# A decoder trunk on one core: the last down products of each feed-forward layer, the first three begun over chunks 0 to 3 of their input and finished over chunks 4 and 5

## The chip, the cores and the metric

The kernel runs on one core of a Trainium2 chip. The metric is device time in microseconds (us) of one execution, the median of several runs. A profile shows one execution in detail. Engine names: PE multiplies matrices (PEld is its loading of weights), DVE, ACT and POOL are the vector, scalar and general-purpose engines, SP issues most of the DMAs.

## What is computed

One inference step of a two-layer trunk over 512 prompt tokens and 32 sample tokens (544 columns), width 1024. Each layer has a mixer (a convolution in layer 0, an attention in layer 1) and then this feed-forward part, whose last line is what the change touches:

```python
def conv_ffn(h, past, w_gate, w_up, w_dw, b_dw, w_down):
    g = h @ w_gate
    ext = jnp.concatenate([past, g], axis=1)
    g_conv = causal_dwconv(ext, w_dw, b_dw)
    out = (jax.nn.silu(g_conv) * (h @ w_up)) @ w_down
    return out, ext[:, -(FFN_CONV_WIDTH - 1):]
...
    x = x + out            # layer 0: then the norm and mixer of layer 1
...
y = rms_norm(x, norm_final)  # layer 1: then the final norm, and y is stored
```

The hidden width is 2816, 22 chunks of 128.

## The kernel before

Activations lie transposed: 128 channels on the partitions, tokens along the free axis, cut in two stretches, SA (columns 0 to 255) and SB (256 to 543, 288 wide). Every matrix product is made of three matmuls per chunk of 128 inputs, because both operands are split into a high and a low part: high weights by high input, high weights by low input, low weights by high input (L459, L460, L461 in `gemm`). A weight block of 128 output channels sits in a slot. ACT writes its high part `whi` (L369) and DVE its low part `wlo` (L372) from a raw block that SP has loaded (L332); when the second block of a raw has been split, its buffer takes the next load.

`ffn` walks over the 22 hidden chunks in passes of 4, 6, 6 and 6 (`PASSES`). For a pass it computes gates and ups, multiplies them into a hidden tile `h`, and splits that into `HH` (ACT, L1596) and `HL` (DVE, L1597), one chunk of 544 columns at a time. Those are the inputs of the down products, which add into the residual `xT`. A list scheduler (`Plan`) sets the order of all this by estimated costs, except for the down products of the last pass, 8 groups for 8 output chunks, which are written out after the plan in program order. There nk is 6: each group runs over hidden chunks 16 to 21, called chunks 0 to 5 below. On every engine the instructions run in the order in which the program issues them.

In layer 0 those last products go through `Wide.stream`, first all 8 groups on SA, then all 8 on SB. Three further slots are prepared in the SA stream after groups 0, 1 and 2. In layer 1 they go through `add_group` and `run_group`, 4 groups at a time: SA then SB for output chunks 0 to 3, SB then SA for 4 to 7. Each group sums into a bank of PSUM (`acc`, four of them in turn); DVE then adds the bank to `xT` (L1687 in layer 0, L1239 in layer 1: the eviction), and a norm object is fed. `Norm.feed` has ACT square the chunk and DVE add it up. In layer 1 `Final.feed` also has ACT write the scaled chunk `xg` (L1725), and PE transposes it (`yt`, L1740) some steps later.

What is to be done "some steps later" waits in a deque `side`. `gemm` takes one entry off it at each of four places in a group: with nk = 6 these come after chunks 1, 2, 4 and 5.

## Time and profile before

| what | value |
|---|---|
| time, median of 3 runs | 1290.41 us (1287.6 to 1290.61) |
| the profiled execution's own time | 1289.36 us |
| its span, first to last instruction | 1287.7 us |
| PE busy | 1270.2 us, 99% of the span |
| DVE busy | 980.4 us, 76% |
| ACT busy | 713.5 us, 55% |
| mean granted PE clock | 0.997 of full speed |
| last down products of layer 0, SA stream | 555.0 to 573.7 us |
| last down products of layer 1 | 1235.5 us to the end of the last group near 1279 us |

A line of the timeline reads: start in us, duration in us, engine, line of the kernel, operation, output<-input, shape, and in brackets how long the engine had been idle and what released it. Matmuls overlap in PE: a matmul of 256 columns is listed with 0.28 us, but a new one starts every 0.12 us, so the spacing of the starts is what one costs.

### The profile page before, as it was taken

To read this page: it belongs to the slowest core of one execution; us is meant where nothing else is said; L and a number is where in the kernel's file an instruction comes from. 1 tells how busy PE (TensorE), PEld (TensorE's weight loads), DVE (VectorE), ACT (ScalarE), POOL (GpSimd) and SP (SyncE) were. 2 spreads that over 40 slices of the span, in tenths; PEclk is the share of its full clock that TensorE was granted. 3 is DMA by queue.
4 is the path that set the end of the run, shared out by engine and by line. 5 is a ranking of instruction groups with operands and counts; after the bars stand their busy time and mean duration, and the time that the engine had idled before them with its cause. 6 is when DMAs were issued, how large, how long until landed. Compare 5 with 4: busy or idle time off the path is not lost.

```text
span 1287.7 us, 26497 instructions
## 1 busy us (share of the span) xinstructions
PE 1270.2 (99%) x10860; PEld 1215.5 (94%) x10860; DVE 980.4 (76%) x1671; ACT 713.5 (55%) x1440; POOL 152.4 (12%) x289
## 2 busy tenths in 40 slices
PE   9999999999999999999999999999999999999997
PEld 8997789999999999999988888889999999999997
DVE  6899875979987877768366586756988987887864
ACT  7596574645644545445366587754645555455453
POOL 4000014101001000000142123100111011000000
PEclk9999999999999999999999999999999999999999
DMA  8465233133232223244553445333133233233221
GB/s 225 123 175 140 83 100 114 34 92 107 91 117 91 91 93 115 67 133 141 175 159 120 140 140 175 104 113 99 50 100 92 93 114 115 67 116 94 80 76 70
DMA packets 119402, 142.38 MB, mean 111 GB/s; under 512 B 5357, under 2 KB 110469, under 8 KB 119010
## 3 DMA queue, kind: packets, MB, share of 16 engines
q1 hardware_dynamic: 110350, 111.89, 28.1%
q0 software_dynamic: 8640, 28.78, 7.1%
q8 instruction: 85, 1.39, 0.5%
q14 instruction: 35, 0.29, 0.1%
q10 hardware_dynamic: 292, 0.02, 0.0%
HBM read 129.34 MB, written 12.18 MB: 110 GB/s over the span
## 4 chain that ended last, share of the span: by engine, by line
PE 85%; DVE 10%; issue 2%; ACT 1%; DMA 1%; DVEq 0%; POOL 0%; ACTq 0%; POOLq 0%
PE acc L1545 5%; PE acc L1543 5%; PE acc L1544 5%; PE acc L700 4%; PE acc L701 4%; PE acc L702 3%; PE acc L459 3%; PE acc L460 3%; PE acc L461 3%; PE tr L1544 3%; PE tr L1543 3%; PE tr L1545 3%; PE av L1341 3%; PE acc L1969 3%; PE av L1343 3%; PE av L1342 3%
## 5 line engine op out<-in xcount | busy, mean ns | idle before, releaser
L372 DVE TENSOR_TENSOR wlo<-raw,whi 128x1024 fp32r<-128x1024 f32 (+2 forms) x245 | 257.4, 1052 | 46.0 <-ACT whi L369 44.5
L369 ACT CAST whi<-raw 128x1024 fp32r<-128x1024 f32 (+2 forms) x245 | 223.5, 914 | 117.1 <-PE av L1342 24.6
L700 PE MATMUL acc<-XH,whi 128*128 128x288 f32 (+1 forms) x384 | 114.5, 298 | 0.0
L701 PE MATMUL acc<-XL,whi 128*128 128x288 f32 (+1 forms) x384 | 110.9, 289 | 0.1
L702 PE MATMUL acc<-XH,wlo 128*128 128x288 f32 (+1 forms) x384 | 110.4, 288 | 0.1
L1969 PE MATMUL acc<-XH,whi 128*128 128x256 f32 (+1 forms) x264 | 82.8, 314 | 0.6 <-ACT XH L2274 0.6
L1543 PE MATMUL acc<-TH,whi 128*128 128x272 f32 x288 | 82.9, 288 | 0.0
L1545 PE MATMUL acc<-TH,wlo 128*128 128x272 f32 x288 | 82.8, 288 | 0.0
L1544 PE MATMUL acc<-TL,whi 128*128 128x272 f32 x288 | 82.7, 287 | 0.0
L1579 ACT COPY G<-acc 128x272 f32<-128x272 f32 (+1 forms) x72 | 26.7, 371 | 94.9 <-PE acc L1545 94.9
L1341 PE MATMUL av<-HH,whi 128*128 128x288 f32 x256 | 76.2, 298 | 0.2
L1970 PE MATMUL acc<-XL,whi 128*128 128x256 f32 (+1 forms) x264 | 76.2, 289 | 0.1
L1971 PE MATMUL acc<-XH,wlo 128*128 128x256 f32 (+1 forms) x264 | 75.9, 287 | 0.0
L1342 PE MATMUL av<-HL,whi 128*128 128x288 f32 x256 | 75.5, 295 | 0.0
L1343 PE MATMUL av<-HH,wlo 128*128 128x288 f32 x256 | 75.3, 294 | 0.0
L700 PEld LDWEIGHTS acc<-XH,whi 128*128 128x128 f32 x384 | 72.2, 188 | 2.8 <-issue 1.6
L701 PEld LDWEIGHTS acc<-XL,whi 128*128 128x128 f32 x384 | 72.3, 188 | 1.0 <-DVE XL L952 0.3
L702 PEld LDWEIGHTS acc<-XH,wlo 128*128 128x128 f32 x384 | 72.2, 188 | 0.3 <-DVE wlo L372 0.3
L1341 PE MATMUL tr<-HH,whi 128*128 128x256 f32 x256 | 71.9, 281 | 0.0
L1342 PE MATMUL tr<-HL,whi 128*128 128x256 f32 x256 | 71.9, 281 | 0.0
L1343 PE MATMUL tr<-HH,wlo 128*128 128x256 f32 x256 | 71.5, 279 | 0.0
L1482 DVE SCALAR_TENSOR_TENSOR cv<-G,fprm,cv 128x560 f32<-128x560 f32 x88 | 69.5, 797 | 0.5
(405 smaller groups left out, 4395.5 us busy)
## 6 DMA issues: line engine op xcount, KB each, us to landing
raw<-in_ffn_w_gate_dram SPq DMA_DIRECT2D x22, 1024.0 KB
raw<-in_ffn_w_up_dram SPq DMA_DIRECT2D x22, 1024.0 KB, 5.4
raw<-in_ffn_w_down_dram SPq DMA_DIRECT2D x24, 768.0 KB, 4.7
raw<-in_attn_w_qkv_dram SPq DMA_DIRECT2D x12, 1024.0 KB, 7.9
raw<-in_conv_w_in_dram POOLq DMA_DIRECT2D x6, 1024.0 KB, 7.8
rep<-glu SPq DMA_DIRECT2D x36, 142.0 KB, 3.7
raw<-in_conv_w_out_dram POOLq DMA_DIRECT2D x4, 1024.0 KB, 6.0
raw<-in_ffn_w_down_dram SPq DMA_DIRECT2D x8, 512.0 KB, 3.4
```

What stands on the lines that cost most here:

```text
L369: act.copy(hi[:, k, :], src[:, k])
L372: dve.tensor_tensor(lo[:, k, :], src[:, k], hi[:, k, :], op=ALU.subtract)
L700: pe.matmul(o, hi[:, k, :], XH[:, k, c0:c0 + n], start=(k == 0), stop=False)
L701: pe.matmul(o, hi[:, k, :], XL[:, k, c0:c0 + n], start=False, stop=False)
L702: pe.matmul(o, lo[:, k, :], XH[:, k, c0:c0 + n], start=False, stop=(k == NC - 1))
L1341: pe.matmul(o, hi[:, j + k, :], xh, start=(start and k == 0), stop=False, **kw)
L1342: pe.matmul(o, hi[:, j + k, :], xl, start=False, stop=False, **kw)
L1343: pe.matmul(o, lo[:, j + k, :], xh, start=False, stop=(stop and k == len(xs) - 1), **kw)
L1543: pe.matmul(o, hi[:, j + k, :], xh, start=(start and k == 0), stop=False, **kw)
L1544: pe.matmul(o, hi[:, j + k, :], xl, start=False, stop=False, **kw)
L1545: pe.matmul(o, lo[:, j + k, :], xh, start=False, stop=(k == 3), **kw)
L1969: pe.matmul(o, hi[:, k, :], XH[:, k, c0:c0 + n], start=(k == 0), stop=False)
```

## The change

`AHEAD = 3`. For the first stretch of the last products, `begin` takes three of the four banks and runs groups 0, 1 and 2 over chunks 0 to 3 (`ready = nk - 2`), 12 matmuls each, one group after the other. Then the groups are run as before, but 0, 1 and 2 only over chunks 4 and 5, 6 matmuls each; from group 3 on nothing is split. This is done for SA in layer 0 and for SA of output chunks 0 to 3 in layer 1. No instruction is added or removed. The begun parts take nothing off `side`, so that groups 0, 1 and 2 have two places each instead of four.

```diff
+AHEAD = 3
-    def gemm(pt, st, slot, xh, xl, places=None):
+    def gemm(pt, st, slot, xh, xl, places=None, ks=(0, NF)):
-        for k in range(nk):
+        for k in range(max(0, ks[0]), min(nk, ks[1])):
+    def begin(n, ready, s0, st, xh, xl):
+
+        pts = [bank("acc", uid("acc")) for _ in range(n)]
+        for i, pt in enumerate(pts):
+            gemm(pt, st, s0 + i, xh, xl, None, (0, ready))
+        return pts
...
+        begun = begin(AHEAD, ready, s0, order[0], xh, xl) if ready else []
...
-                pt = bank("acc", uid("acc"))
+                k0 = ready if begun else 0
+                pt = begun.pop(0) if begun else bank("acc", uid("acc"))
...
-                gemm(pt, st, s0 + i, xh, xl, places if hooked else None)
+                gemm(pt, st, s0 + i, xh, xl, places if hooked else None, (k0, NF))
...
-                last.stream(st)
+                last.stream(st, ready=0 if st is SB else nk - 2)
...
-                add_group(c4, HH, HL, after, hooked=True, order=(SB, SA) if c4 else (SA, SB))
+                add_group(c4, HH, HL, after, hooked=True, order=(SB, SA) if c4 else (SA, SB), ready=0 if c4 else nk - 2)
```

Place 1, PE in layer 0, the start of the last products. `acc_7003` is the bank of group 0, `acc_7028` before and `acc_7004` after that of group 1, `acc_7005` that of group 2; a bracket names the engines whose semaphores a matmul waits for. Before, the end of chunk 3 and then chunks 4 and 5 of group 0:

```order
L459 MATMUL acc_7003<-HH_3021,whi_6882 128x256
L460 MATMUL acc_7003<-HL_3022,whi_6882 128x256
L461 MATMUL acc_7003<-HH_3021,wlo_6883 128x256
L459 MATMUL acc_7003<-HH_3021,whi_6882 128x256 [waits Activation_49]
L460 MATMUL acc_7003<-HL_3022,whi_6882 128x256 [waits DVE_49]
L461 MATMUL acc_7003<-HH_3021,wlo_6883 128x256
L459 MATMUL acc_7003<-HH_3021,whi_6882 128x256 [waits Activation_49]
L460 MATMUL acc_7003<-HL_3022,whi_6882 128x256 [waits DVE_49]
L461 MATMUL acc_7003<-HH_3021,wlo_6883 128x256
L459 MATMUL acc_7028<-HH_3021,whi_6918 128x256
```

Now, the end of chunk 3 of group 2, and chunk 4 of group 0 behind it (the lines are one higher):

```order
L460 MATMUL acc_7005<-HH_3021,whi_6952 128x256
L461 MATMUL acc_7005<-HL_3022,whi_6952 128x256
L462 MATMUL acc_7005<-HH_3021,wlo_6953 128x256
L460 MATMUL acc_7003<-HH_3021,whi_6882 128x256 [waits Activation_49]
L461 MATMUL acc_7003<-HL_3022,whi_6882 128x256 [waits DVE_49]
L462 MATMUL acc_7003<-HH_3021,wlo_6883 128x256
L460 MATMUL acc_7003<-HH_3021,whi_6882 128x256 [waits Activation_49]
```

The four waits for `HH` and `HL` of chunks 4 and 5 stand 24 matmuls later on PE. DVE, ACT, POOL and SP have the same rows in the same order there as before.

Place 2, PE in layer 1, the transposes of the first chunk. `xg` is output chunk 0 after its eviction, scaled by ACT; `yt` are banks for the transposes. Before, in group 1 (`acc_15164`), 15 matmuls behind the end of group 0:

```order
L461 MATMUL acc_15164<-HH_11157,wlo_15056 128x256
L1740 MATMUL yt_15180<-ident,xg_15159 128x128 [waits Activation_49]
L1740 MATMUL yt_15181<-ident,xg_15159 128x128
L459 MATMUL acc_15164<-HH_11157,whi_15055 128x256
L460 MATMUL acc_15164<-HL_11158,whi_15055 128x256
```

Now, in group 2 (`acc_15140`), 9 matmuls behind the end of group 0, of which six finish group 1 (`acc_15139`):

```order
L462 MATMUL acc_15139<-HH_11157,wlo_15056 128x256
L460 MATMUL acc_15140<-HH_11157,whi_15089 128x256
L461 MATMUL acc_15140<-HL_11158,whi_15089 128x256
L462 MATMUL acc_15140<-HH_11157,wlo_15090 128x256
L1752 MATMUL yt_15205<-ident,xg_15185 128x128 [waits Activation_49]
L1752 MATMUL yt_15206<-ident,xg_15185 128x128
L460 MATMUL acc_15140<-HH_11157,whi_15089 128x256
```

The transposes of the next chunks, and the copies of transposed rows on DVE and ACT (`yrow`), move behind by up to 18 matmuls; from the second group of output chunks 4 to 7 on, every engine has its old order.

More of the change, by code (lines that the diff above doesn't have):

```diff
@@ L472, in take_due, with run_group @@
             side.extend(due.popleft())
-    def run_group(n, xh, xl, evac, hooked=False, order=(SA, SB)):
+    def begin(n, ready, s0, st, xh, xl):
[3 more added lines that the diff above has]
+        return pts
+    def run_group(n, xh, xl, evac, hooked=False, order=(SA, SB), ready=0):
         s0 = slot_no[0]
         slot_no[0] += n
+        begun = begin(AHEAD, ready, s0, order[0], xh, xl) if ready else []
         for st in order:
@@ L499, in __init__, with stream @@
             self.cm, self.pool = open_pool(uid("more"))
-        def stream(self, st, hooked=True):
+        def stream(self, st, hooked=True, ready=0):
             last = st is SB
+            begun = begin(AHEAD, ready, self.s0, st, self.xh, self.xl) if ready else []
             for i in range(NC):
-                pt = bank("acc", uid("acc"))
+                k0 = ready if begun else 0
+                pt = begun.pop(0) if begun else bank("acc", uid("acc"))
                 places = [[some]] * 4
@@ L507, in stream @@
                     places[0] = [take_due, some]
-                gemm(pt, st, self.s0 + i, self.xh, self.xl, places if hooked else None)
+                gemm(pt, st, self.s0 + i, self.xh, self.xl, places if hooked else None, (k0, NF))
                 if not last and i < self.lead:
@@ L1229, in tile_trunk, with add_group @@
     due.append(nrm.steps(SB))
-    def add_group(c4, xh, xl, norm, bias_row=None, hooked=True, order=(SA, SB)):
+    def add_group(c4, xh, xl, norm, bias_row=None, hooked=True, order=(SA, SB), ready=0):
         def evac(i, st, pt):
@@ L1243, in evac @@
                 norm.feed(st, c)
-        run_group(4, xh, xl, evac, hooked=hooked, order=order)
+        run_group(4, xh, xl, evac, hooked=hooked, order=order, ready=ready)
     def ffn(l, before, after):
```

## The prediction

> **What bounds the kernel now.** The page's head and its chain of work that ended last come first.

> ```profile
> span 1287.7 us, 26497 instructions
> PE 1270.2 (99%) x10860; PEld 1215.5 (94%) x10860; DVE 980.4 (76%) x1671; ACT 713.5 (55%) x1440; POOL 152.4 (12%) x289
> PE 85%; DVE 10%; issue 2%; ACT 1%; DMA 1%; DVEq 0%; POOL 0%; ACTq 0%; POOLq 0%
> ```

> PE is the bound nearly everywhere. A change of order in PE's work can win only what PE waits, and the view of waits, for PE, says how much of that is due to the inputs in question:

> ```profile
> PE acc L460 <- DVE HL L1597: 2.1, 4, 0.9
> ```

> Four waits of matmul L460 for `HL`, 2.1 us together. The timeline of PE shows the two of layer 0; the first row is the first matmul of group 0, the last one the first of the SB stream:

> ```profile
> 555.04 0.36 PE L459 MATMUL acc<-HH,whi 128*128 128x256 f32 x1
> 555.24 0.28 PE L460 MATMUL acc<-HL,whi 128*128 128x256 f32 x1
> ...
> 556.54 0.28 PE L459 MATMUL acc<-HH,whi 128*128 128x256 f32 x1
> 556.99 0.39 PE L460 MATMUL acc<-HL,whi 128*128 128x256 f32 x1 [0.17 <-DVE HL L1597]
> 557.21 0.28 PE L461 MATMUL acc<-HH,wlo 128*128 128x256 f32 x1
> 557.33 0.28 PE L459 MATMUL acc<-HH,whi 128*128 128x256 f32 x1
> 558.49 0.39 PE L460 MATMUL acc<-HL,whi 128*128 128x256 f32 x1 [0.88 <-DVE HL L1597]
> 558.72 0.28 PE L461 MATMUL acc<-HH,wlo 128*128 128x256 f32 x1
> ...
> 573.69 0.29 PE L459 MATMUL acc<-HH,whi 128*128 128x288 f32 x1
> ```

> From 558.72 to 573.69 there are 127 starts without a wait: 14.97 / 127 = 0.118 us each. That is the unit below. What PE waits for is made by ACT and DVE, in this order:

> ```profile
> 556.21 0.72 DVE L1597 TENSOR_TENSOR HL<-h,HH 128x544 fp32r<-128x544 f32 x1
> 556.38 0.64 ACT L1596 CAST HH<-h 128x544 fp32r<-128x544 f32 x1
> 556.85 0.95 DVE L372 TENSOR_TENSOR wlo<-raw,whi 128x768 fp32r<-128x768 f32 x1
> 557.72 0.72 DVE L1597 TENSOR_TENSOR HL<-h,HH 128x544 fp32r<-128x544 f32 x1
> 559.04 0.42 DVE L1687 TENSOR_TENSOR xT<-acc,xT 128x256 f32<-128x256 f32 x1 [0.60 <-PE acc L461]
> ```

> `HL` of chunk 4 ends at 556.93, `HH` of chunk 5 at 557.02, `HL` of chunk 5 at 558.44, held up by a `wlo` between the two. None of these waits for the down products, so they stay where they are when PE does other work meanwhile.

> Layer 1 has the same picture:

> ```profile
> 1235.72 0.28 PE L460 MATMUL acc<-HL,whi 128*128 128x256 f32 x1
> ...
> 1237.02 0.28 PE L459 MATMUL acc<-HH,whi 128*128 128x256 f32 x1
> 1237.47 0.39 PE L460 MATMUL acc<-HL,whi 128*128 128x256 f32 x1 [0.17 <-DVE HL L1597]
> ...
> 1237.81 0.28 PE L459 MATMUL acc<-HH,whi 128*128 128x256 f32 x1
> 1238.97 0.38 PE L460 MATMUL acc<-HL,whi 128*128 128x256 f32 x1 [0.88 <-DVE HL L1597]
> 1239.20 0.28 PE L461 MATMUL acc<-HH,wlo 128*128 128x256 f32 x1
> ```

> **The change part by part.** *The two waits of layer 0.* Counted by starts and not by idle time, they cost more than the view of waits says. 556.54 to 556.99 is 0.45, 0.33 above the unit; the next start comes 0.22 later, 0.10 above; 557.33 to 558.49 is 1.16, 1.04 above; the next 0.23, 0.11 above. Sum 1.58 us. The 0.10 behind each wait goes with it, since there PE starts up again from an empty pipe.

> They go if the input is there when PE now comes to it. 36 matmuls stand ahead instead of 12. Counted from the second at 555.24, the matmul that needs `HL` of chunk 5 is the 41st and would start at 555.24 + 39 x 0.118 = 559.84, and `HL` is ready at 558.44: 1.4 us to spare. For chunk 4 (38th, 559.49 against 556.93) it is 2.6 us. So both waits go whole: -1.58 us.

> *What is late next in layer 0.* Group 0 ends later. Its last matmul, at 558.72 so far, is the 42nd and starts at 559.96; its eviction, 0.32 behind that (558.72 to 559.04), moves from 559.04 to 560.28. Its bank is next used by group 4, whose first matmul is the 73rd, at 563.6: 2.9 us of cover for a 0.42 us eviction. Groups 0, 1 and 2 now end 0.71 apart (6 x 0.118) and not 2.1, and between their evictions DVE has the three `wlo` of the slots 5, 6 and 7 to make, 0.95 each as above. So the three evictions and three `wlo` take DVE from 560.28 to about 564.4 (3 x 0.42 + 3 x 0.95 = 4.1). Slot 5 is first needed by the 91st matmul, at 565.7, slot 7 by the 127th at 570. Cost nothing; without that cover PE would wait what DVE is behind.

> SP's next load, the first of the qkv weights, waits for the first of these `wlo`, so it moves from 560.36 to about 561.6:

> ```profile
> 560.36 0.37 SPq L332 DMA_DIRECT2D raw<-in_attn_w_qkv_dram  x1
> raw<-in_attn_w_qkv_dram SPq DMA_DIRECT2D x8, 1024.0 KB, 8.6
> 577.12 1.03 ACT L369 CAST whi<-raw 128x1024 fp32r<-128x1024 f32 x1
> ```

> With 8.6 us to landing (median of these loads, second row) it is there at 570.2. The cast that reads it would come 1.58 earlier than 577.12, at 575.5. Cover 5.3 us, cost nothing. POOL's queue and its DMAs are not touched.

> *Does the gain of layer 0 reach the end?* After the SA stream the chain that ended last runs over DVE until PE takes over again:

> ```profile
> 576.28 0.47 DVE xT L1687
> 592.16 0.40 PE acc L459
> ```

> It enters DVE with the eviction of the first SB group, which waits for PE, so that the norm behind it, and all that follows up to layer 1, starts earlier with PE. I take the whole 1.58.

> *Layer 1.* The same sum, 0.33 + 0.10 + 1.04 + 0.11 = 1.58 us (the restart rows are as in layer 0). `HL` of chunk 5 is needed at 1235.72 + 39 x 0.118 = 1240.32, and its wait so far ended at 1238.97 at the latest: 1.35 to spare. But the transposes now come nearer to what they read:

> ```profile
> 1239.51 0.42 DVE L1239 TENSOR_TENSOR xT<-acc,xT 128x256 f32<-128x256 f32 x1 [0.59 <-PE acc L461]
> 1239.97 0.51 ACT L1725 ACTIVATE xg<-xT,prm 128x256 f32<-128x256 f32 x1 [1.09 <-DVE xT L1239]
> 1240.39 0.40 ACT L1726 ACTIVATE sq<-xT 128x256 f32<-128x256 f32 x1
> 1241.09 0.38 PE L1740 MATMUL yt<-ident,xg 128*128 128x128 f32 x2
> ```

> Group 0's last matmul started at 1239.20, the eviction 0.31 later, `xg` 0.46 after that and ended 0.51 on: 1.28 us in all, and the transposes came 1.89 after that matmul. Now that matmul is the 42nd, at 1240.43, so `xg` ends at 1241.71. Nine matmuls stand between, so the transposes could start at 1240.43 + 10 x 0.118 = 1241.61. They wait 0.1, and with the hand-over from ACT to PE (`HL` ended at 558.44, its matmul started at 558.49) some 0.15 to 0.2. Bounds: nothing at all, and 0.5 if the square (0.40 behind `xg` on ACT) had to be done too. I take 0.2, nearest to the rows' own sum. The next chunk's transposes come 9 matmuls into group 3, over 0.9 us after their `xg`; later ones have moved away from what they read. The final stretch has its old order and starts from PE:

> ```profile
> 1273.14 0.51 PE ms L1759 x6
> ```

> so it shifts as a whole. The row copies on DVE and ACT that move behind an eviction there fill no queue that PE waits for: cost nothing.

> *Sum.* 1.58 + 1.58 - 0.2 = 2.96 us off. The profiled execution's own time is 1289.36 (span 1287.7 and 1.7 around it), which gives 1286.4. The median of the runs, 1290.41, is 1.05 above it, which gives 1287.45. I go from their middle, 1289.9: 1286.9 us, 0.23% less.

> [...] Changing banks costs PE nothing in this trace, with `av` and `tr` two banks of products that are open side by side:

> ```profile
> 548.87 0.29 PE L1545 MATMUL av<-XH,wlo 128*128 128x272 f32 x1
> 549.00 0.29 PE L1543 MATMUL tr<-TH,whi 128*128 128x272 f32 x1
> ```

> 0.13 us from one to the other, as within a bank. [...]

> **The rivals.** B: layer 0's gain is lost on the way, because something between 592 and 1235 us runs by its own clock (a DMA or a POOL gather). For it: 15% of the chain is not PE's. Against it: the chain comes back to PE each time. Then only layer 1 gains: 1289.9 - 1.38 = 1288.5.

> C: the change doesn't do what it says, as a wait for chunk 4 or 5 still stands ahead of the begun groups, or `HL` comes later than now. For it: nothing but that DVE's chain ahead is tight (556.21 to 558.44 without a gap). It would have to slip by 1.4 us. Then 1289.9.

> D: slower, by the clock. At the kernel's start PE ran at half speed, later at full:

> ```profile
> 1.30 4.23 PE L994 MATMUL warm<-zero 128*128 128x256 bf16 x19 [1.30 <-DVE zero L634]
> 8.31 1.91 PE L994 MATMUL warm<-zero 128*128 128x256 bf16 x16
> ```

> 4.23 / 19 = 0.223 against 1.91 / 16 = 0.119 us for 256 columns: 0.103 more for each. If the 54 matmuls of groups 0 to 2 ran so in both layers, that is 108 x 0.103 = 11.1 - 2.96 = 8.2 slower, 1298.1. It decides from 29 slow matmuls on (2.96 / 0.103). [...]

> E: more than the sum, if PE's wait for an eviction in the SB stream of layer 0 also goes:

> ```profile
> PE acc L459 <- DVE xT L1687: 1.1, 1, 1.1
> ```

> 1289.9 - 2.96 - 1.1 = 1285.8. Against it: that wait is the end of the DVE chain from 576.28, which keeps its distance to PE.

> **How the numbers follow.** Chances: my sum 0.68, B 0.12, C 0.05, D 0.04, E 0.11. The runs before spread over 3.0 us (1287.6 to 1290.61), so half of that to either side of 1286.9 is my sum's own range, 1285.4 to 1288.4. To leave out no more than 2 in 10 I reach down below E, to 1284.8, and up to between B and C with that scatter, 1290.2. A measurement of this kernel can tell about 0.3%, 3.9 us, from no change. My sum lies 0.9 us short of that, so scatter carries some one in five of its cases over the line (0.14); with most of E that is 0.23 for faster. Slower is D, 0.04. The rest, 0.73, is within 0.3%.

> **What the profile after would show.** PE's starts from group 0 to group 3 of the SA stream 0.12 apart with no wait for `HL`; the stream from its first matmul to the first of SB 17.1 us long and not 18.65 (573.69 - 555.04). In layer 1 one short wait of a `yt` transpose for `xg`, 0.1 to 0.2. The time from layer 0's last SB matmul to layer 1's first down product unchanged; if it is longer by what layer 0 won, B is right. Spacings of 0.2 in groups 0 to 2 would be D, a wait for `HL` at the 38th or 41st matmul C. I am wrong in size if the restart of 0.1 behind each wait returns without a wait, which would take 0.4 from the sum.

## The result, and the profile after

The changed kernel took 1285.64 us (median of 9 runs, 1284.88 to 1289.31) against 1289.45 us for the kernel before next to it (9 runs, 1287.6 to 1291.52): a ratio of 0.9973, 95% interval 0.9964 to 0.9982, so 0.27% faster. Forecast were 1286.9 us and 0.23%. The profiled execution took 1284.92 us. The head of its page:

```profile
span 1283.2 us, 26496 instructions
PE 1267.9 (99%) x10860; PEld 1213.6 (95%) x10860; DVE 979.9 (76%) x1671; ACT 713.7 (56%) x1440; POOL 152.9 (12%) x289
```

One of the nine runs, that of 1289.31, is 3.7 us above the median, at a mean granted clock of 0.996; the other eight have 0.998.

The span is 4.5 us shorter, and the forecast had 2.96. Both traces hold 10860 matmuls, so the n-th start of one can be set against the n-th start of the other; "shift" below is after less before, read off at places by the time they have before. In the experiments it is the step in this difference at the place named.

| place (us, before) | 534 | 560 | 576 | 620 | 843 | 869 | 1234 | 1248 | 1279 |
|---|---|---|---|---|---|---|---|---|---|
| shift (us) | -0.07 | -1.65 | -1.63 | -1.59 | -1.58 | -3.12 | -3.10 | -4.45 | -4.48 |

Three steps, then: 1.58 at layer 0's last products, 1.53 near 859 us, and 1.35 at layer 1's last products. The first and the third are the change, 2.93 together. The second stands at a place that the change doesn't touch.

The view of waits of after, for PE, has no `HL` any more. The wait of the SB stream for an eviction is still there (the lines of `gemm` moved by 1, those behind it by up to 12):

```profile
PE acc L460 <- DVE xT L1699: 1.1, 1, 1.1
...
PE acc L462 <- DVE wlo L373: 0.7, 1, 0.7
PE av L2277 <- DVE XL L2287: 0.7, 1, 0.7
PE acc L1981 <- ACT XH L2286: 0.6, 1, 0.6
```

The timeline of after, in order of time, answers to the rows of the forecast. The first matmul of group 0, then those that take chunk 4 and 5 of `HL` (the 38th and 41st), the eviction of group 0 with the first `wlo` behind it, SP's load, the third of these `wlo`, the first matmul of the SB stream and the cast that reads SP's load:

```profile
554.97 0.36 PE L460 MATMUL acc<-HH,whi 128*128 128x256 f32 x1
555.17 0.28 PE L461 MATMUL acc<-HL,whi 128*128 128x256 f32 x1
...
559.44 0.28 PE L461 MATMUL acc<-HL,whi 128*128 128x256 f32 x1
559.56 0.28 PE L462 MATMUL acc<-HH,wlo 128*128 128x256 f32 x1
559.68 0.28 PE L460 MATMUL acc<-HH,whi 128*128 128x256 f32 x1
559.80 0.28 PE L461 MATMUL acc<-HL,whi 128*128 128x256 f32 x1
...
560.24 0.42 DVE L1699 TENSOR_TENSOR xT<-acc,xT 128x256 f32<-128x256 f32 x1 [1.87 <-PE acc L462]
560.58 0.95 DVE L373 TENSOR_TENSOR wlo<-raw,whi 128x768 fp32r<-128x768 f32 x1
561.56 0.37 SPq L333 DMA_DIRECT2D raw<-in_attn_w_qkv_dram  x1
563.47 0.95 DVE L373 TENSOR_TENSOR wlo<-raw,whi 128x768 fp32r<-128x768 f32 x1
572.05 0.30 PE L460 MATMUL acc<-HH,whi 128*128 128x288 f32 x1
575.49 1.03 ACT L370 CAST whi<-raw 128x1024 fp32r<-128x1024 f32 x1
```

The second start is 0.20 behind the first, as it was before (555.04 and 555.24). From there on no start is more than 0.12 behind the one ahead, and the stream from first to first is 17.08 us long. In layer 1 the transposes wait once:

```profile
1238.43 0.28 PE L462 MATMUL acc<-HH,wlo 128*128 128x256 f32 x1
1238.71 0.44 PE L1752 MATMUL yt<-ident,xg 128*128 128x128 f32 x2
1238.90 0.36 PE L460 MATMUL acc<-HH,whi 128*128 128x256 f32 x1
1239.11 0.29 PE L461 MATMUL acc<-HL,whi 128*128 128x256 f32 x1
```

The step near 859 us is one of the clock. The stretches of before there, with the columns of us, then for PE, PEld, DVE, ACT and POOL the busy time and number of instructions, then the granted PE clock, DMA share and GB/s:

```profile
855.57:858.98 3.41, 2.04 (x15) 1.47 (x16) 1.07 (x4) 0.94 (x4) 0.00 (x0) 1.00 0.01 5
858.98:862.40 3.42, 3.42 (x19) 3.42 (x18) 1.61 (x4) 1.21 (x3) 0.00 (x0) 0.50 0.00 0
```

and of after at the same work:

```profile
852.18:855.60 3.42, 2.73 (x43) 2.31 (x39) 0.29 (x1) 0.57 (x3) 0.00 (x0) 1.00 0.26 112
855.60:859.01 3.41, 2.67 (x20) 2.27 (x19) 1.75 (x6) 1.18 (x4) 0.00 (x0) 1.00 0.00 0
859.01:862.42 3.41, 3.41 (x28) 3.41 (x27) 1.34 (x4) 0.89 (x3) 0.00 (x0) 1.00 0.02 5
```

Before, PE ran at half clock for 3.41 us, behind a stretch of equal length in which it was busy 60% of the time: layer 1's attention ends there, and PE waits 0.69 us for an `XL` and 0.61 us for an `XH`:

```profile
856.19 0.66 PE L2265 MATMUL av<-w,vtok 128*64 128x128 f32 x8 [0.69 <-DVE XL L2275]
858.00 0.38 PE L1969 MATMUL acc<-XH,whi 128*128 128x256 f32 x1 [0.61 <-ACT XH L2274]
```

After has the same two waits (0.69 and 0.61), but they fall into two stretches, 80% and 78% busy, and there is no half clock. Is this step part of what the change does, or luck of one execution? The second half of the experiments is about that. A stretch of half clock lowers the mean clock of an execution by 0.0013 (half of 3.41 in 1285). In the 14 profiles the mean is 0.997 in the three with such a stretch inside the program, and 0.998 or 0.999 in the others. So the runs can be sorted by it: at 0.997 or less ("low"), or above. The mean does not say where in the execution a stretch stands; only a profile does.

### The profile page after: what moved, and what is told of

The parts are those of the page before. It is cut to its first block, busy times and chain, and to the rows that moved or that the text cites. A ratio compares the mean times of both kernels' runs of the same rounds, so it can differ in the third digit from the quotient of the medians.

```text
span 1283.2 us, 26496 instructions
## 1 busy us (share of the span) xinstructions
PE 1267.9 (99%) x10860; PEld 1213.6 (95%) x10860; DVE 979.9 (76%) x1671; ACT 713.7 (56%) x1440; POOL 152.9 (12%) x289
## 4 chain that ended last, share of the span: by engine, by line
PE 84%; DVE 11%; issue 2%; ACT 1%; DMA 1%; DVEq 0%; SPq 0%; POOL 0%; ACTq 0%; POOLq 0%
PE acc L1557 5%; PE acc L1555 5%; PE acc L1556 5%; PE acc L712 4%; PE acc L713 4%; PE acc L714 3%; PE acc L460 3%; PE acc L462 3%; PE acc L461 3%; PE tr L1557 3%; PE tr L1556 3%; PE tr L1555 3%; PE av L1353 3%; PE acc L1981 3%; PE av L1355 3%; PE av L1354 3%
## 6 DMA issues: line engine op xcount, KB each, us to landing
raw<-in_ffn_w_gate_dram SPq DMA_DIRECT2D x22, 1024.0 KB
raw<-in_ffn_w_up_dram SPq DMA_DIRECT2D x22, 1024.0 KB
raw<-in_attn_w_qkv_dram SPq DMA_DIRECT2D x12, 1024.0 KB
raw<-in_conv_w_in_dram POOLq DMA_DIRECT2D x6, 1024.0 KB, 7.9
raw<-in_conv_w_out_dram POOLq DMA_DIRECT2D x4, 1024.0 KB, 5.8
```

## Experiments: the parts of the change

**Layer 0 alone.**

```diff
-add_group(c4, HH, HL, after, ..., ready=0 if c4 else nk - 2)
+add_group(c4, HH, HL, after, ...)
```

> The begun groups in layer 0 only. Both theories: PE's starts at layer 0's last products lie 1.58 us nearer together, and layer 1 is as before. Theory (grid): the half-clock stretch of 3.41 us that the profile of before has at 859 us comes when a lull in PE's work falls wholly into one window of a grid that is fixed to the program's start; 1.58 us earlier the lull is split over two windows, so that the stretch is gone (another 1.53 us). Then the span is 1284.6 (1287.7 - 1.58 - 1.53) and the runs lie 3.1 us below those runs of before that have the stretch, 1.6 below those that have not. Rival (chance): the stretch comes and goes by itself, whatever the shift; then the mean gain is 1.6 us and this kernel has the stretch as often as before.

1286.36 us, ratio 0.9984 (0.9975 to 0.9993). None of 11 runs was low, against 13 of 33 of the kernel before beside them, and the profile has no half clock inside the program and a span of 1284.7. That speaks against chance, and for the place of the lull. The shift is -1.59 at layer 0's last products and 0.0 at layer 1's, where the two waits are left:

```profile
PE acc L461 <- DVE HL L1609: 1.1, 2, 0.9
```

**Layer 1 alone.**

```diff
-last.stream(st, ready=0 if st is SB else nk - 2)
+last.stream(st)
```

> The begun groups in layer 1 only. Both theories: nothing moves up to 1235 us, then 1.58 - 0.22 = 1.36 us are won, the 0.22 being a wait of the first transposes for their scaled chunk. Theory (grid): up to layer 1 PE stands on the grid as before, so the half-clock stretch at 859 us is there as often as in before, and the span is 1286.3 in a profile that has it. The gains of this and of the run with layer 0 alone then sum to the whole gain of the change. Rival (chance): the stretch is there in some other share of the runs.

1287.93 us, ratio 0.9991 (0.9982 to 1.0). The shift is 0 at layer 0 and -1.35 at layer 1, so that the two halves, 1.59 and 1.35, add up to the whole. Low runs came, 8 of 11, as the grid theory asked. But its half clock at 859 us isn't in the profile, though that is one of the low ones: there the one such stretch begins at 157.62 us (shown in the last section), and the two waits at the end of the attention lie in two stretches that are 80% and 78% busy. So a low run need not have its stretch at the attention.

**Two groups begun and not three.** `AHEAD = 2`.

> Two groups begun instead of three, in both layers. The last HL is ready at 558.44 in layer 0; the matmul that needs it is then the 29th, at 558.43, so PE waits 0.05 us (hand-over) and perhaps starts up again for 0.1: 1.42 to 1.58 us won per layer instead of 1.58. In layer 1 the first transposes stand 12 matmuls behind the end of group 0 instead of 9 (1.42 us; the scaled chunk takes 1.28 us), so the 0.2 us wait for it is gone. Theory: PE at the last products -1.45 in layer 0 and -1.45 in layer 1, the whole within 0.2 us of the changed kernel. Rival (three are needed, because the waits need more room than the starts say): a wait of over 0.3 us for HL is left in each layer, and the gain is under 1.2 us per layer.

1286.02 us, ratio 0.9976 (0.9967 to 0.9985). The view of waits lists none for `HL` here either; the shifts are -1.42 and -1.40. What the third group bought is seen in the starts at the matmul that takes `HL` of chunk 5, the 29th here, 0.05 and 0.10 above the unit:

```profile
559.40 0.28 PE L460 MATMUL acc<-HH,whi 128*128 128x256 f32 x1
559.57 0.39 PE L461 MATMUL acc<-HL,whi 128*128 128x256 f32 x1
559.79 0.28 PE L462 MATMUL acc<-HH,wlo 128*128 128x256 f32 x1
```

That is the 0.05 and the 0.1 of the expectation. In layer 1 the same is lost, and the `yt` transposes, 12 matmuls behind the end of group 0, don't wait.

**Only chunk 5 held back.** `ready = nk - 1` in both places.

> The changed kernel with only chunk 5 held back (ready = nk - 1): groups 0, 1 and 2 begin with 15 matmuls each and end with 3. Theory: the matmuls for chunk 4 of group 0 come as early as before the change, so that wait stays with 0.33 + 0.10 us, and only that of chunk 5 goes, 1.04 + 0.11 = 1.15 us in each layer. In layer 1 the first yt transposes now come 12 matmuls behind the end of group 0 and not 9, 0.35 us more room, so their wait of 0.2 goes too: -2.3 us against the kernel before, in two steps of 1.15. Rival: DVE is what sets it, and a wait removed at chunk 4 comes back elsewhere, so that holding back one chunk is worth as much as two (2.9), or the split in itself costs something, which 18 changes of group instead of 6 would show as less than 2.0.

1286.16 us, ratio 0.9981 (0.9972 to 0.999). The shifts are -1.17 and -1.10. What is left is chunk 4's wait, with 0.44 to its matmul and 0.23 from there to the next, where before had 0.45 and 0.22:

```profile
556.16 0.28 PE L460 MATMUL acc<-HH,whi 128*128 128x256 f32 x1
556.60 0.39 PE L461 MATMUL acc<-HL,whi 128*128 128x256 f32 x1 [0.17 <-DVE HL L1609]
556.83 0.28 PE L462 MATMUL acc<-HH,wlo 128*128 128x256 f32 x1
```

By the steps in the trace, 2.27 together, the theory's 1.15 for chunk 5, and so 0.43 for chunk 4, hold, and the rival (2.9, or under 2.0) falls. The median alone would not say so: it lies 1.6 us under that of before's runs above 0.997, 1287.80.

**The input earlier instead of the matmul later.** In the kernel before, the `wlo` that stands between the two `HL` is issued behind the second:

```diff
...
+            keep = f2 + 2 == NF
...
-                low_h(f2 + i, k0, hs[i])
+            lows = [low_h(f2 + i, k0, hs[i]) for i in range(2)]
+            if keep:
+                prepare(slots[3] + SPLIT_BUFS, lows)
```

> The kernel before with one DVE instruction moved in each layer: the wlo that stands between HL of chunk 4 and HL of chunk 5 comes behind HL of chunk 5. PE's order is that of before. Theory: HL of chunk 5 then starts when HH of chunk 5 is ready (557.02 in layer 0) and not when that wlo has ended (557.72 as the start of HL), 0.65 us earlier, so PE's wait for it shrinks from 1.04 to about 0.4, the rest stays: -0.65 us in each layer, -1.3 us together. The eviction of group 0 then waits some 0.2 to 0.4 us for the wlo, which nothing feels. Rival: HL of chunk 5 is bound by HH or by h, and PE waits as before: 0. Or the wlo behind it comes late for PE's group in that slot, and the gain is lost again: 0 or above.

1286.91 us, ratio 0.9988 (0.9979 to 0.9997). The shifts are -0.56 and -0.66, where -0.65 each was expected. The timeline:

```profile
556.95 0.73 DVE L1598 TENSOR_TENSOR HL<-h,HH 128x544 fp32r<-128x544 f32 x1 [0.22 <-ACT HH L1597]
557.13 0.28 PE L459 MATMUL acc<-HH,whi 128*128 128x256 f32 x1
557.60 0.95 DVE L372 TENSOR_TENSOR wlo<-raw,whi 128x768 fp32r<-128x768 f32 x1
557.73 0.39 PE L460 MATMUL acc<-HL,whi 128*128 128x256 f32 x1 [0.33 <-DVE HL L1598]
557.96 0.28 PE L461 MATMUL acc<-HH,wlo 128*128 128x256 f32 x1
```

Now `HL` waits for `HH`, 557.13 to 557.73 is 0.48 above the unit, and the restart behind it is unchanged. So DVE's order was 0.6 of the 1.58. Beginning three groups is worth more, because it also covers the 1.0 us that the two inputs still cost PE in this order.

## Experiments: the half clock

**The attention later.** To the kernel before, 12 matmuls are added in layer 0, so that all of layer 1 comes 1.6 us later:

```diff
+                if last and i == 0 and self.hold:
+                    for _ in range(12):
+                        pe.matmul(pt[:, :st[1]], W.w[self.s0][0][:, 0, :], self.xh[:, 0, st[0]:st[0] + st[1]],
+                                  start=True, stop=False, skip_group_check=True)
                 gemm(pt, st, self.s0 + i, ...)
```

> The kernel before, with 12 more matmuls of 288 columns at the head of layer 0's SB stream (their sums are overwritten): 12 x 0.133 = 1.6 us more work on PE. Theory (grid): PE's lull moves from 853.5-858.9 to 855.1-860.5 us, over two windows of the grid, the half-clock stretch at 859 us is gone (-1.53), and the kernel with more work is not slower than before where before has the stretch: 0.1 us, span 1287.8. Rival (chance): 1.6 us slower, span 1289.3, with the stretch as often as before.

1289.53 us, ratio 1.001 (1.0001 to 1.0019): the added work cost 1.58 us where it stands, and the median rose by 0.7 only (by 1.6 over before's runs above 0.997, 1287.92). There is no half clock near 859 us in the profile, and none of 11 runs was low, against 13 of 33 runs of before. But the clock does not step at times fixed to the span's start: a stretch of half clock begins at 858.98 us in the profile of before, and at 857.47 in that of the changed kernel with 12 matmuls (below), 1.51 us apart, where a stretch lasts 3.41. So this run alone could not say whether the place mattered.

**The changed kernel again.**

> The changed kernel once more, unchanged. Theory: the gain is what the waits for HL cost by starts, 1.58 us in layer 0 and 1.36 us in layer 1 (1.58 less 0.22 for the wait of the first yt transposes), 2.94 us; what the first comparison showed beyond that (3.8 us between the medians) are executions of the kernel before that lost 1.5 us to a stretch of half granted clock. Then the runs of both kernels with a mean clock of 0.998 lie 2.5 to 3.2 us apart, and runs at 0.997 or less lie 1.3 to 2 us above those of their own kernel. Rival 1: the change also keeps the clock up by itself, because PE pauses less; then the changed kernel has next to no run at 0.997 or less, again, while the kernel before has a third or more of them. Rival 2: the change is worth 3.5 us or more at equal clock; then the distance at 0.998 is 3.5 or more.

1284.66 us (5 runs, 1284.53 to 1284.93), ratio 0.9967 (0.9954 to 0.998). None was low, of before's 29 runs 17. The runs of before above 0.997 have a median of 1287.80, so at equal clock the change is worth 3.1 us, beside 2.94 by the shifts; before's low runs have 1289.42, 1.6 more. The theory's distance holds and rival 2 falls. Its 1.3 to 2 us for a low run could be seen in the kernel before alone; the changed kernel's one low run, in the first comparison, is 3.7 above the median of its own runs there, more than one stretch explains. Rival 1's count came in too: the changed kernel does have next to no low runs. The same kernel took 1285.64 us in the first comparison, so medians of different groups of runs can lie 1 us apart.

**Work in the pause.** The kernel before with six zero matmuls where PE waits for `XH`:

```diff
-    zero = conv.tile([P, 2 * P], BF16, name="zero")
+    zero = base.tile([P, 2 * P], BF16, name="zero")
...
+                if fill and k == NC - 1:
+                    for _ in range(6):
+                        pe.matmul(o, zero[:, :P], zero[:, :n], start=False, stop=False)
```

> The kernel before with six more matmuls of 256 columns (zero weights by zeros, added into an open bank, so that the sums stay the same) in a pause of PE at the end of layer 1's attention: PE had nothing from 857.24 to 858.00 there, waiting for XH. In the profile of before half granted clock set in at 858.98, behind a stretch of 3.41 us in which PE was busy 60% of the time. Theory: such a low stretch is what brings the half clock, and with 0.7 us more work it is 80%; then the profile has no half clock near 859, no or few runs at a mean clock of 0.997 or less, and the median is that of before's runs at 0.998, some 1 us under before's median if these are again a third or more of its runs. The six cost 0 to 0.1 us. Rival: the half clock comes from elsewhere (a level over many us, another place in the program such as the convolution); then the share of runs at 0.997 or less is as in before, and the median is 0 to 0.2 us above it.

1288.34 us, ratio 0.9997 (0.9988 to 1.0006); none of 11 was low, of before's 29 beside them 17. The six cost nothing in the trace (shift +0.24 ahead of them, -1.29 behind, where 1.53 is the missing half clock), but the median is 0.5 above that of before's runs above 0.997, and so only 0.6 under before's whole. The stretch that was 60% busy, between two steps of the clock, is 80% now (second row):

```profile
852.46:855.87 3.41, 3.26 (x44) 2.88 (x42) 0.00 (x0) 0.11 (x1) 0.00 (x0) 1.00 0.74 311
855.87:859.28 3.41, 2.73 (x22) 2.05 (x23) 1.07 (x4) 0.86 (x4) 0.00 (x0) 1.00 0.01 5
```

**The changed kernel with the pause put back, and moved by a whole period.** The 12 matmuls above, now in the changed kernel; then 26 of them (3.4 us) in the changed kernel, and in the kernel before; then the 12 and the six zero matmuls together.

> The changed kernel with 12 matmuls of 288 columns more on PE, into the bank of the first SB group of layer 0's last products ahead of its own (that group clears the bank, so the sums stay the same). All of layer 1 comes 1.5 to 1.6 us later by it, that is where it was before the change. Open is why so many runs of the kernel before, and so few of the changed one, have a stretch of half clock. Theory: the clock is set anew every 3.41 us, at times that lie within about 1 us the same from the start of each execution, and only if one such time falls in the 0.6 us in which the 3.41 us behind it hold the pause at the end of the attention does the half clock come; the change moved that pause by 1.6 us out of it. Then a third or more of these runs are at a mean clock of 0.997 or less, as of before, and the median is 1287 to 1288. Rival 1: those times are free of the program's start; then about 0.6 / 3.41 = 18% of the runs, one to three of eleven, of this kernel as of any other. Rival 2: the change of layer 0 itself keeps the clock up; then none, and 1286.2 to 1286.6.

> The same with 26 matmuls, 3.4 to 3.5 us, one period of the clock's steps. Theory of times that keep to the program's start: the pause comes to the same place in the period as in the changed kernel, so that no or one run is at 0.997 or less; median 1288.1 to 1288.5. Rival 1, free times: one to three of eleven. Were half the runs low here as in the last kernel, the added matmuls would be the cause, and not where the pause falls.

> The kernel before with the 26 matmuls. Theory of times that keep to the program's start: the pause is one period later and so at the same place in the period as in the kernel before, a third or more of the runs at 0.997 or less; median 1291.5 to 1292.5. Rival 1: one to three of eleven. Rival 2, that layer 0 as it was before brings the half clock: as before too, a third or more, so this run parts theory from rival 1 alone.

> The changed kernel with the 12 matmuls of 288 columns in layer 0 and with the six zero matmuls in the pause at the end of layer 1's attention. Theory: the pause no longer holds 0.7 us without work, so wherever it falls no half clock comes: none of the runs at 0.997 or less, median 1286.2 to 1286.8. If the half clock comes from elsewhere: the same share of low runs as in the kernel with the 12 matmuls alone.

With the pause back at its old place, 5 of 11 runs were low (1287.17 us, ratio 0.999, 0.9981 to 0.9999), and its profile shows the half clock again:

```profile
854.06:857.47 3.41, 2.08 (x22) 1.26 (x18) 1.02 (x4) 0.96 (x4) 0.00 (x0) 1.00 0.01 5
857.47:860.88 3.41, 3.31 (x15) 3.31 (x16) 0.90 (x3) 0.83 (x2) 0.00 (x0) 0.50 0.00 0
```

With the pause also filled, none of 11 was low (1287.95 us, ratio 0.9999, 0.999 to 1.0008). With 26 matmuls the changed kernel had none in 11 (1289.35 us, ratio 1.0006, 0.9997 to 1.0015), and the kernel before 3 of 5 (1295.08 us, ratio 1.0061, 1.0048 to 1.0075). All kernels in one table, by how far the pause stands from its place in the kernel before, as their profiles have it:

| kernel | pause moved by (us) | low runs |
|---|---|---|
| before (13 of 33, 17 of 29, 13 of 27) | 0 | 43 of 89 |
| layer 1 alone | 0 | 8 of 11 |
| change, 12 matmuls | 0.0 | 5 of 11 |
| before, 26 matmuls | +3.4, one period | 3 of 5 |
| `wlo` behind `HL` | -0.5 | 3 of 12 |
| only chunk 5 | -1.1 | 0 of 11 |
| two groups | -1.4 | 1 of 11 |
| layer 0 alone; change (two groups of runs) | -1.6 | 0 of 11; 1 of 14 |
| before, 12 matmuls | +1.6 | 0 of 11 |
| change, 26 matmuls | +1.8 | 0 of 11 |
| filled: before; change, 12 matmuls | 0; +0.9 | 0 of 11; 0 of 11 |

Free times (18% for each kernel) don't fit 43 of 89 beside 2 of 69 for the six kernels whose pause stands 1.1 to 1.8 off. That the change itself keeps the clock up by having fewer waits falls too: with the same waits removed, the low runs are back once 12 matmuls move the pause back, and the kernel before, with all its waits, has none when the pause is 1.6 later. So by these counts it matters where the pause falls. That it is there matters too: in the kernel before it kept its place when it was filled, and the low runs went. The other filled kernel does not show this by itself, because a wait further ahead moved its pause by 0.9 us.

Two limits remain. Where the half clock stood is known for the profiled executions alone: of the three low ones, two have it at the end of the attention (before; change with 12 matmuls) and one at 157.62 us (layer 1 alone). And in the kernel before with 26 matmuls, whose pause is moved by a whole period, two of the three low runs have a clock of 0.995, lower than one stretch makes it in the profiles, and the profiled execution is not a low one. So the 3 of 5 weigh little.

Some medians don't fit the sums. Against before's runs above 0.997, 26 matmuls should have given the changed kernel about 0.5 us more, and gave 1.5; the kernel before with them should have stood 3.4 higher and stood over 6.5. Of two groups the runs above 0.997 lie 2.1 under, for 2.8 by the shifts, and those of only chunk 5 lie 1.6 under, for 2.27. In the profiles part of this is at places that the edits don't touch. Ahead of layer 0's last products the work of the two kernels with 26 matmuls is 0.97 and 1.28 us later than before's, and that of two groups 1.07. Only chunk 5 loses 0.27 again behind 1262 us. The kernel before with 26 matmuls loses 0.97 more between 900 and 1234 us and 0.78 at layer 1's last products, with two waits that before does not have:

```profile
PE acc L459 <- ACT HH L1600: 0.7, 1, 0.7
PE tr L1547 <- ACT h L1615: 0.7, 1, 0.7
```

The change with 12 matmuls and the fill stood 1.2 to 1.8 above what was expected; its trace has the second of these waits, and one for a gather of the cache, at 664.98 us, which is what moved its pause:

```profile
PE t L2096 <- DMA xT<-in_cache_k_dram,idx: 1.1, 1, 1.1
...
PE tr L1559 <- ACT h L1627: 0.7, 1, 0.7
```

Why these came was not tried, and stays open.

## Why the forecast was right, point by point

- *The two waits of layer 0, 1.58.* Right: 1.58 and 1.59 measured in three kernels. It was right to count by starts. The view of waits gives 1.1 us in a layer (2.1 in both); the other 0.5 is restart and hand-over. The restart did not come back anywhere.
- *The cover.* Right: forecast 1.4 us to spare for `HL` of chunk 5; the 41st matmul now starts at 559.80 and no wait is seen. That two groups, one group of 1.42 us less, leave 0.05 of the wait and a restart of 0.10 fits it.
- *What is late next.* The eviction was forecast for 560.28 and came at 560.24, the third `wlo` ended at 564.42 (forecast 564.4), SP's load came at 561.56 (561.6) and its cast at 575.49 (575.5). None of it reached PE.
- *Layer 0's gain reaches the end.* Right: the shift stays between -1.58 and -1.65 from 560 to 843 us. Rival B falls for this change, though the wait for a gather in the last experiment shows that its mechanism exists here.
- *Layer 1, 1.38.* 1.35 in two profiles of the changed kernel and in layer 1 alone. The `yt` wait is 1238.43 to 1238.71, 0.16 above the unit, and a restart of 0.05: 0.21, where 0.2 was taken. `xg` ended 0.06 ahead of it.
- *Rivals C, D and E.* No wait for `HL` is left. In the three groups of layer 0 no spacing of 0.2 is seen but that of the first two starts, which before has too. The wait of 1.1 us for an eviction stayed as it was, and the shift is -1.63 on both sides of it. So no run shows the slow clock in groups 0 to 2 that D supposes, and the changes of bank between them cost nothing: 0.12 us from start to start there too.
- *The sum, 2.96.* 2.93 measured.
- *The step that failed is the base.* The forecast laid the sum on 1289.9, as if an execution of before differed from one of after by the change alone. About half of the executions of before are low, and the profiled one has 1.5 us of half clock at the end of the attention. With that pause moved by 1.58 us, next to no execution of the changed kernel is low (1 of 14). From the profiled execution's 1289.36 the whole sum was 2.96 + 1.53, which gives 1284.9; it took 1284.92. In the medians it is some 0.7 us, 3.8 less the 3.1 at equal clock. Another 0.45 of what the forecast was off is the sample: nine runs of before have 1289.45, where the forecast went from 1289.9. The trace of before shows the half clock in the table by stretches (0.50 in the row from 858.98), and the forecast did not look there. D named the clock, but in the wrong place and with the wrong sign.

## What to carry to other kernels

A wait of PE is priced by the spacing of starts, with the restart behind it (1.58 us in a layer here, where the view of waits has 1.1), and went whole here when other groups of the same input stood ahead for longer than the input is late. The input is 1.4 us late (558.44, where PE without waits would want it at 557.0); one more group, 1.42 us, left 0.15 of that cost, and two more left none. Before a sum of one or two us is laid on a measured time, look in that execution for what is not in the program, a stretch of lower clock above all; here it came and went with the place of a pause that the change doesn't touch (43 of 89 executions of before low, 1 of 14 of the changed kernel). Then compare traces matmul by matmul: each cause is a step at its own place.

## What the runs showed of the hardware

That 43 of 89 executions of before are low points to a grid that keeps step with the program. A likely reason, an estimate from three profiles and not tried: the work moves with the steps of the clock. In the change with 12 matmuls the step stands 1.51 us ahead of that of before (857.47 against 858.98) and the work 0.95 ahead (the matmul that waits for `XL` at 855.24 against 856.19). In after, both stand within 0.1 us of those of before ahead of the change (the first switch to full at 5.68 against 5.65, the first matmul of group 0 in layer 0 at 554.97 against 555.04).

The busy share alone does not settle it. At the end of the program steps with 58% (from 1278.82 us in before) and 38% (from 1275.43 us in after) brought the half clock. In the profile of layer 1 alone a step with 35% brought the half clock:

```profile
154.20:157.62 3.42, 1.19 (x24) 0.56 (x20) 3.31 (x10) 2.79 (x6) 0.00 (x0) 1.00 0.07 17
157.62:161.03 3.41, 3.41 (x39) 2.17 (x32) 3.41 (x7) 3.41 (x10) 0.65 (x1) 0.50 0.66 169
```

In that of the kernel before with the pause filled a step with 54%, at the same work, did not, though one with 60.0% at the attention had in before:

```profile
156.14:159.55 3.41, 1.84 (x36) 1.40 (x40) 3.32 (x10) 3.41 (x9) 0.00 (x0) 1.00 0.46 128
159.55:163.00 3.45, 3.34 (x65) 2.12 (x60) 2.65 (x7) 3.45 (x11) 0.88 (x1) 1.00 0.31 65
```

What is counted there stays open.
